# Max-unpool on one core: loading x in two transfers instead of one

## Chip, cores and metric

The kernel runs on one core of a Trainium2 chip. The metric is the device time of one execution in microseconds; "the time" below is a median over several executions. A profiled execution also gives a page and a trace; its span, from the first to the last instruction, is about 1.3 us shorter than the time. All runs compared here are at a granted clock of 1.0 (the clock of TensorE, which this kernel doesn't use).

## The reference, cut to what matters

```python
batch, channels, h, w = 16, 64, 32, 32        # x: float32, indices: 0..3
for b, c, i, j in all positions:
    idx = indices[b, c, i, j]
    output[b, c, 2*i + idx // 2, 2*j + idx % 2] = x[b, c, i, j]   # the rest stays 0
```

Each element of x goes to one of four places of a 2 x 2 cell. 1024 images of 32 x 32 become 1024 images of 64 x 64. The indices reach the device as 64-bit integers, so they are 8.4 MB against 4.2 MB of x; the output is 16.8 MB.

## The kernel before

Every partition holds eight whole images: 32 KB of x, 64 KB of indices. VectorE makes the output with `(index == k) * x` for k = 0..3, written with a stride of two, for two images at a time (for the images on either side of the cut in the indices, one at a time). Three loads are issued at the very start of the program, and four stores of 4 MB follow, each as soon as its two images are made.

```python
x_v = x.rearrange("b (ch t) h w -> (b ch) (t h w)", t=T)      # T = 8, N = 1024
...
cut = FIRST * 2 * N                                           # FIRST = 3 images
with Program(nc) as program:
    program.first(nc.sync.dma_start(out=x_t, in_=x_v).then_inc(x_in, 16))
    for half, part in enumerate((slice(0, cut), slice(cut, None))):
        program.first(
            nc.sync.dma_start(out=idx_t[:, part], in_=idx_v[:, part]).then_inc(
                idx_in[half], 16))

    nc.vector.wait_ge(x_in, 16).then_inc(x_in, -16)
    for t in range(T):
        g, k = t // G, t % G                                  # G = 2 images a store
        if t in (0, FIRST):
            half = int(t == FIRST)
            nc.vector.wait_ge(idx_in[half], 16).then_inc(idx_in[half], -16)
        ...                                                   # four operations
        if k + n == G:
            op.then_inc(made, 1)

    for g in range(NG):                                       # NG = 4
        nc.sync.wait_ge(made, g + 1)
        nc.sync.dma_start(out=out_v[g], in_=out_t[g]).then_inc(
            stored if g else stored_0, 16)
```

## Time and profile before

| | before |
|---|---|
| time, median of 3 runs | 71.66 us (71.65 to 72.0) |
| span of the profiled run | 70.2 us |
| VectorE busy | 35.6 us, 51% |
| DMA queue busy, share of 16 engines | 97.5% |
| bytes moved | 29.36 MB |

The prediction below shows the page's main lines. Two more belong beside them. The first is from the waits of the DMA-issuing SyncE, the second from the page's list of groups (busy us and mean ns of one, then the idle time just before and what ended it):

```profile
SPq L146 <- DVE out_t L133: 52.4, 4, 26.8
L133 DVE SCALAR_TENSOR_TENSOR out_t<-idx_t,x_t 128x2048 f32<-128x2048 int32 (+1 forms) x20 | 35.6, 1857 | 19.6 <-DVEq L122 19.6
```

(A q behind an engine's name means its sequencer, the part that waits and issues; L122 is the wait for the first indices.) SyncE waits 52.4 us for VectorE, and VectorE stands idle for 19.6 us before its first operation. Read alone this says that an earlier VectorE would end the kernel earlier. But SyncE only issues; what it issues stands behind the loads in the queue of the 16 DMA engines, and these are what has no gap.

### The profile page before, as it was taken

How to read it: one execution, taken by the hardware profiler on the slowest of the kernel's cores; microseconds unless marked ns; L12 is line 12 of the kernel's file. 1: busy time of each engine (PE TensorE's matmuls, PEld its weight loads, DVE VectorE, ACT ScalarE, POOL GpSimd, SP SyncE). 2: the span in 40 equal slices, each digit the busy share in tenths (PEclk: the TensorE clock that was granted, in tenths of full speed). 3: DMA queues.
4: the chain of work that ended last, by engine and by line, in shares of the span. 5: the costliest groups of instructions: out<-in, count | busy, mean ns of one | idle time of the engine just before them, and what ended most of it. 6: DMA issues, size and time to landing. Idle time of an engine off the chain costs nothing.

```text
span 70.2 us, 72 instructions
## 1 busy us (share of the span) xinstructions
DVE 35.6 (51%) x20; POOL 0.2 (0%) x4
## 2 busy tenths in 40 slices
DVE  0000000000089999999999999999999400000000
POOL 1000000000000000000000000000000000000000
DMA  9769695999988899969989696979799796969792
GB/s 280 317 299 597 299 578 243 448 448 448 597 373 373 373 513 583 397 299 485 411 355 541 299 597 299 578 317 560 336 392 504 317 578 299 597 299 560 336 504 93
DMA packets 1008, 29.36 MB, mean 418 GB/s; under 512 B 112, under 2 KB 112, under 8 KB 112
## 3 DMA queue, kind: packets, MB, share of 16 engines
q1 hardware_dynamic: 1008, 29.36, 97.5%
HBM read 12.58 MB, written 16.78 MB: 418 GB/s over the span
## 4 chain that ended last, share of the span: by engine, by line
DVE 46%; DVEq 4%; issue 1%
DVE out_t L133 46%; DVEq L183 4%
## 5 line engine op out<-in xcount | busy, mean ns | idle before, releaser
L133 DVE SCALAR_TENSOR_TENSOR out_t<-idx_t,x_t 128x2048 f32<-128x2048 int32 (+1 forms) x20 | 35.6, 1857 | 19.6 <-DVEq L122 19.6
L169 POOL MEMSET const-bfloat16-1.0<- 128x1 bf16 x1 | 0.1, 101 | 0.0
L169 POOL MEMSET const-uint8-127<- 128x1 uint8 x1 | 0.1, 101 | 0.0
L169 POOL MEMSET const-float32-0.0<- 128x1 f32 x1 | 0.1, 98 | 0.2 <-issue 0.2
L169 POOL MEMSET const-float32-1.0<- 128x1 f32 x1 | 0.1, 98 | 0.0
## 6 DMA issues: line engine op xcount, KB each, us to landing
out_dram<-out_t SPq DMA_DIRECT2D x4, 4096.0 KB, 13.8
idx_t<-in_indices_dram SPq DMA_DIRECT2D x1, 5120.0 KB, 30.6
x_t<-in_x_dram SPq DMA_DIRECT2D x1, 4096.0 KB, 12.1
idx_t<-in_indices_dram SPq DMA_DIRECT2D x1, 3072.0 KB, 19.0
```

What stands on the lines that cost most here:

```text
L133: op = nc.vector.scalar_tensor_tensor(out=o_c[:, k : k + n, :, pidx // 2, :, pidx % 2], in0=idx_c[:, t : t + n], scalar=pidx, in1=x_c[:, t ...
L169: nc = _bacc.Bacc("TRN2", target_bir_lowering=False, num_devices=1)
L183: with _tile.TileContext(nc) as tc:
```

## The change

The first image of each partition (rows of 4 KB) is loaded in a transfer of its own, the other seven (rows of 28 KB) in a second. VectorE still waits for both. As VectorE can't start sooner and the queue has no other gap, a gain could only lie in the start-up: a first transfer with short rows might get the engines going sooner.

```diff
-        program.first(nc.sync.dma_start(out=x_t, in_=x_v).then_inc(x_in, 16))
+        for part in (slice(0, N), slice(N, None)):
+            program.first(
+                nc.sync.dma_start(out=x_t[:, part], in_=x_v[:, part]).then_inc(x_in, 16)
+            )
...
-        nc.vector.wait_ge(x_in, 16).then_inc(x_in, -16)
+        nc.vector.wait_ge(x_in, 32).then_inc(x_in, -32)
```

## The prediction

> **What bounds the kernel now.** I began with the page's strip of 40 slices and its table of DMA queues, to see whether an engine or the transfers fill the span:
>
> ```profile
> span 70.2 us, 72 instructions
> DVE  0000000000089999999999999999999400000000
> DMA  9769695999988899969989696979799796969792
> DMA packets 1008, 29.36 MB, mean 418 GB/s; under 512 B 112, under 2 KB 112, under 8 KB 112
> q1 hardware_dynamic: 1008, 29.36, 97.5%
> ```
>
> VectorE works only in the middle of the span, while the one DMA queue is busy for 97.5% of what 16 engines could be. The single low slices in the DMA strip come from the way packets are booked to slices: over longer windows they vanish. So I asked for the sums of seven stretches (length, busy time of VectorE and GpSimd, granted clock, DMA share, GB/s), cut where the stages change:
>
> ```profile
> 0.00:1.03 1.03, 0.00 (x0) 0.20 (x4) 1.00 0.13 32
> 1.03:2.00 0.97, 0.00 (x0) 0.00 (x0) 1.00 1.56 473
> 2.00:3.10 1.10, 0.00 (x0) 0.00 (x0) 1.00 0.76 328
> 3.10:12.80 9.70, 0.00 (x0) 0.00 (x0) 1.00 0.99 426
> 12.80:31.30 18.50, 11.74 (x7) 0.00 (x0) 1.00 1.02 439
> 31.30:69.50 38.20, 23.86 (x14) 0.00 (x0) 1.00 0.99 425
> ```
>
> From 3.10 us to the end, through loads and stores alike, the transfers run at 425 to 439 GB/s with a share of about 1. There is no gap between the last load and the first store, nor between stores. Only the first 3.1 us differ. The chain of waits names VectorE (46%), because it follows instructions and stops at the last store's issue; it does not see that this store then stands in a queue. The timeline and the table of DMA issues show the standing:
>
> ```profile
> 19.56 35.59 DVE L133 SCALAR_TENSOR_TENSOR out_t<-idx_t,x_t 128x2048 f32<-128x2048 int32 x20 [19.56 <-DVEq L122]
> 28.49 27.03 SPq L146 DMA_DIRECT2D out_dram<-out_t  x4
> x_t<-in_x_dram SPq DMA_DIRECT2D x1, 4096.0 KB, 12.1
> idx_t<-in_indices_dram SPq DMA_DIRECT2D x1, 5120.0 KB, 30.6
> ```
>
> The second index load is issued in the first 1.4 us and lands 30.6 us after its issue, about 31.6. The first store is issued at 28.49, some 2.7 us before the first of the 16 engines finishes its loads (the completion records of that load begin at 31.19). The later stores are issued at 37.6, 46.4 and 55.2 us, while their predecessors finish at 40.9, 50.5 and 60.2, so the lead grows to 5.0 us. VectorE's first operation, which ends its wait at 19.56, waits for the first index load (line 122 is that wait), not for x: x has landed at 12.1 us.
>
> Below the views lie the trace's records of single packets. Each of the 16 engines carries 56 data packets, one for each row of a transfer: 24 KB packets take 912 ns, 32 KB packets 1213 ns and 40 KB packets 1514 ns, the same to a nanosecond or two everywhere but in the first round. Seven completion packets of 4 bytes take 9 ns each. Successive packets overlap by about 3.5 ns. The slowest engine: its first packet ends at 3.311 us, then 39 packets of 32 KB, 8 of 24 KB, 8 of 40 KB and 7 completions give 47.31 + 7.30 + 12.11 + 0.06 less 0.22 of overlap, or 66.56 us: it ends at 69.87. The last completion is seen at 70.21. So **the time is the start-up of 3.3 us, plus a fixed sum of packets, plus 0.34 us at the end**; the measured run time adds about 1.3 us outside the span (71.56 against 70.24 in the profiled run).
>
> **What the Trainium skill says.** "DMA: Bandwidth & Descriptors", section "Queues, rings and completion order": one transfer is split over up to 16 engines, and each consumes its descriptors in ring order, with no barrier between data descriptors. The trace agrees: an engine starts the first index packet straight behind its last x packet. "SBUF — State Buffer", section "The DMA setup-cost knee (why "@ 1 MiB" ≠ asymptote)", gives every transfer a fixed cost of roughly 2 us and advises the largest single transfer. Applied blindly this would charge 2 us for the new transfer; the trace of before decides against it for queued transfers, since a boundary between two of them costs one 9 ns packet. The first page's "Why a DMA increments its semaphore by 16 and not by 1" warns about transfers that share a semaphore: an intermediate count doesn't tell which bytes have landed, only the full one does. The changed kernel waits for 32, both parts in full, so nothing starts on half of x, rightly or wrongly.
>
> **The change, part by part.** It removes one transfer of 128 rows of 32 KB and adds two: 128 rows of 4 KB, then 128 of 28 KB. Bytes, the index loads, all 20 VectorE operations and all four stores are unchanged and in the same order; the comparison of the two instruction orders shows one more copy on SyncE and nothing else.
>
> 1. Packets. From 912 ns for 24 KB and 1213 for 32 KB, a byte costs 301/8192 = 0.0367 ns and a packet 912 - 903 = 9 ns besides. A 4 KB packet should take 9 + 150.5 = 160 ns, a 28 KB one 9 + 1053.5 = 1063: together 1222 against 1213. Less the overlap of 3.5 ns, each extra packet costs 5.5 ns. Per engine there are 8 more data packets and one more completion: 9 x 5.5 = 50 ns. This lies on the bounding queue: **+0.05 us**.
> 2. One more issue. Successive issues on SyncE start 0.43 to 0.48 us apart (0, 0.43 and 0.91 us), so the last index load is issued at about 1.4 us instead of 0.9. It is not needed before about 20 us: 0. The second part of x is issued at 0.43, and, by the first transfer's 1.03 to 2.00 us from issue to packets, could begin between 1.5 and 2.4. The small part occupies each engine 8 x 0.156 = 1.25 us, from about 1.8 until about 3.1. No gap: 0.
> 3. VectorE's wait for 32 instead of 16. x lands at about 12.2, the index load that VectorE really waits for at about 19.6: 0. If all loads land 0.05 us later, the operations and the stores' issues shift equally, and the lead of 2.7 us of the first store stays.
> 4. The start-up. This is the only stretch with room. The 16 first packets start between 1.03 and 2.00 us, but take 1.21 to 2.17 us instead of 1.21, and end between 2.95 and 3.31 with no relation to when they started: one that began at 1.05 ended at 2.95, one at 1.14 at 3.31. That looks like a gate which opens for all at 1.7 to 2.1 us (their ends less 1.21). A 4 KB first packet would then simply end about 1.05 us sooner and the next follow: 0.
>
> Sum: +0.05 us, so 71.66 becomes **71.7 us**.
>
> **The rivals.** A: the first packets are slow because they are large, and small ones run at the full rate from the moment they are recorded. The engine that started at 1.14 would gain 0.96 us, but the end is the slowest engine's. The last to start, at 2.00, took 1.265 us, only 0.05 too many, and ended at 69.83; without the excess, 69.77 against 69.87. So with unchanged starting times the gain is at most 0.10 us, less the 0.05: 71.6. For it speaks that first packets are slow at all; against it, that ends do not follow starts.
> B: the spread of starts, 0.97 us, is the making of descriptors, and goes with the bytes of a row. With 4 KB rows it would shrink to an eighth, all engines could start at about 1.2, and up to some 0.9 us would be saved: 70.8. Against: the issues themselves take 383 ns for 32 KB rows, 433 for 24 KB, 432 for 40 KB and 332 to 347 for the stores' 32 KB, which does not follow row size; and the gate would remain.
> C: the gate opens only when the burst of issues is over. Now the third issue ends at 1.34 us, and the gate opens at 1.73 to 2.10. A fourth issue of some 0.43 to 0.48 us moves it to about 2.2 to 2.6: 72.15. Nothing in one trace separates this from a coincidence.
> D: 4 KB pieces at a pitch of 32 KB read slower. If each small packet took twice its 160 ns, 8 x 0.16 = 1.3 us more: 73.0. The skill's "DMA: Bandwidth & Descriptors", section "Latency and other measured facts", reports losses at row pitches above 512 KiB only; the pitch here is 32 KiB, the present packets at that pitch run without loss, and no run yet shows 4 KB ones.
>
> **Range and chances.** The mainline and A lie at 71.6 to 71.7; B could take off up to 0.9, and C add 0.5. Three runs of before already spread from 71.65 to 72.0. I take 71.7 with a range of 71.3 to 72.2, which holds a partial B and all of C. Two per cent is 1.43 us: faster by that much would need more than B in full, so 0.02; slower needs D or something not thought of, so 0.03; within 2%: 0.95.
>
> **What would show it right or wrong.** In the changed profile: 1152 packets, 128 of them between 2 and 8 KB; 4 KB packets near 160 ns and 28 KB ones near 1063; DMA share about 1 from 3.1 us to the end; VectorE's first operation at 19.5 to 19.7 us, still released by the index wait; all stores issued over 2 us before the queue runs dry. If the first packets end before 1.9 us, A or B is right and the gate was the large packet; if they end after 2.4, C. A gap between the two parts of x would refute point 2, longer 4 KB packets past the first would show D. Had VectorE waited at line 120 for x, point 3 would be wrong.

## The result, and the profile after

| | before | changed |
|---|---|---|
| time, median of 6 runs | 71.69 us (71.65 to 72.0) | 71.64 us (71.56 to 71.79) |
| ratio | | 0.9986, 95% interval 0.9965 to 1.0006 |
| span of the profiled run | 70.2 us | 70.3 us |

A ratio is the mean time of one kernel's fast runs over that of the other's in the same rounds, so it is not quite the ratio of the medians. The time is the same.

The page of the changed kernel, packets and queue, then its DMA issues (KB each, us from issue to landing):

```profile
span 70.3 us, 73 instructions
DMA  4997997999988899969989796979999796969793
DMA packets 1153, 29.36 MB, mean 418 GB/s; under 512 B 129, under 2 KB 129, under 8 KB 257
q1 hardware_dynamic: 1152, 29.36, 97.7%
idx_t<-in_indices_dram SPq DMA_DIRECT2D x1, 5120.0 KB, 30.3
x_t<-in_x_dram SPq DMA_DIRECT2D x1, 3584.0 KB, 11.8
x_t<-in_x_dram SPq DMA_DIRECT2D x1, 512.0 KB, 3.7
```

There are 144 packets more on the queue: 128 of 4 KB and 16 completions of 4 bytes. (The one packet more in the first count is an instruction fetch.) The queue is as busy as before. The same stretches as in the prediction:

```profile
0.00:1.03 1.03, 0.00 (x0) 0.20 (x4) 1.00 0.08 8
1.03:2.00 0.97, 0.00 (x0) 0.00 (x0) 1.00 0.78 135
2.00:3.10 1.10, 0.00 (x0) 0.00 (x0) 1.00 1.40 581
3.10:12.80 9.70, 0.00 (x0) 0.00 (x0) 1.00 1.01 433
12.80:31.30 18.50, 11.63 (x7) 0.00 (x0) 1.00 1.02 439
31.30:69.50 38.20, 23.96 (x14) 0.00 (x0) 1.00 0.99 425
```

A packet is booked to the stretch in which it starts, with all its bytes. That is why the second stretch fell from 473 to 135 GB/s and the third rose from 328 to 581: the engines now start 4 KB there instead of 32, and the difference follows. It is no sign of slower loading. From 3.1 us on little has changed: 433, 439 and 425 GB/s against 426, 439 and 425. The timeline:

```profile
0.00 0.86 SPq L111 DMA_DIRECT2D x_t<-in_x_dram  x2
0.90 0.95 SPq L115 DMA_DIRECT2D idx_t<-in_indices_dram  x2
19.67 35.59 DVE L136 SCALAR_TENSOR_TENSOR out_t<-idx_t,x_t 128x2048 f32<-128x2048 int32 x20 [19.67 <-DVEq L125]
28.59 27.03 SPq L149 DMA_DIRECT2D out_dram<-out_t  x4
```

VectorE starts at 19.67 instead of 19.56 and is still released by line 125, the wait for the first indices, not by line 120, the wait for x. Everything behind it is about 0.1 us later.

**A measure for the start-up.** To compare it between traces I add up, over the 16 engines, the usual durations, less the overlap of 3.5 ns each, of the packets that they had done by 6 us (of one under way, the share done), divide by 16 and take this from 6 us. The result is the moment at which, on average, the engines would have had to begin at their full pace: below, "flow begins". Beside it stand the end of an engine's last packet, as the mean of the 16 and the slowest, and the "late stalls": the mean excess per engine, over their usual duration, of packets that start after 6 us. The trace doesn't name a packet's engine; it follows from which packet ends where the next begins. All are worked out from the packet records of the traces.

| trace | first rows | flow begins | late stalls | mean end | slowest end |
|---|---|---|---|---|---|
| before | 32 KB | 1.88 us | 0.01 us | 69.66 us | 69.87 us |
| before, again | 32 KB | 1.96 | 0.01 | 69.74 | 69.99 |
| changed | 4 KB | 1.78 | 0.12 | 69.72 | 69.96 |
| changed, again | 4 KB | 1.81 | 0.05 | 69.67 | 69.94 |

The means of the two traces each: flow begins 0.13 us earlier (1.92 to 1.79). What remains of the mean end when start and late stalls are taken off is 67.77 in both traces before, and 67.83 and 67.82 in the changed ones: 0.05 us more for the additional packets. The late stalls cost 0.08 us more; most of that is 40 KB packets near 29.3 us (0.10 and 0.03 us an engine in the two traces). The sum is nil: 69.70 and 69.70.

### The profile page after: what moved, and what is told of

Read it like the earlier page. It is cut to its first block, busy times and chain, and to the rows that moved or that the text cites. A ratio compares the mean times of both kernels' runs of the same rounds, so it can differ in the third digit from the quotient of the medians.

```text
span 70.3 us, 73 instructions
## 1 busy us (share of the span) xinstructions
DVE 35.6 (51%) x20; POOL 0.2 (0%) x4
## 4 chain that ended last, share of the span: by engine, by line
DVE 46%; DVEq 4%; issue 1%
DVE out_t L136 46%; DVEq L186 4%
```

## The experiments

Twelve further runs were made (three of them repeats), each timed in rounds with the kernel before on the same chip. All gave correct results. The theory at the outset: the DMA engines bound the time, a packet more costs 5.5 ns and nothing else, and the only thing that could be won is a part of the start-up. The edits of the runs with eight transfers, with a tiny first one, with the large part first and with ScalarE are shown against the changed kernel; the others against the kernel before, unless another is named. Where a cut in an edit leaves something out, three dots stand.

### The two kernels again

No edit.

> The kernel before, against itself, to have the noise of times and of the start-up in a second trace. All theories: ratio 1.000 within 0.2%, 1008 packets, all 32 KB packets but the first round at 1213 ns. The first packets should again end at about 2.9 to 3.3 us whatever their start, if a gate that opens for all engines at 1.7 to 2.1 us is a property of this program; if the ends spread anew by more than 0.3 us, the start-up of one trace is chance, and differences of 0.1 to 0.2 us between single traces carry nothing.

Measured: 71.67 us, ratio 0.9991 (0.9968 to 1.0015). The first packets ended at 2.77 to 3.44 us; the prediction's trace had 2.95 to 3.31. The ends of a single engine are thus partly chance, and the slowest engine of one trace carries nothing; the mean over 16 engines moved by 0.08 us between the two traces, and differences below that are not read. By the expectation's own yardstick (ends that spread anew by more than 0.3 us) the start-up of one trace is chance, so what is said of it below rests on several traces that agree.

> The changed kernel again. Theory 1 (the split costs 9 extra packets per engine at 5.5 ns, 0.05 us, and the start-up gives back up to 0.2 us of it, so the sum is nil): ratio 0.997 to 1.002, first packets ending at 1.5 to 2.2 us as in the first trace, earlier on average by about 0.2 us once their length is taken off. Rival (pure chance in the start-up): first packets, less 159 ns, at 1.7 to 2.1 us as in the kernel before. In both, stalls of the 40 KB packets at 29.2 to 29.5 us, seen on ten engines in the first trace of the changed kernel (up to 361 ns), should not recur at the same size if they are chance; if they recur they belong to the change.

Measured: 71.63 us, ratio 0.999 (0.996 to 1.0021). Flow begins at 1.81 us, again outside the range of the kernel before. Stalls of 40 KB packets came again at 29.2 to 29.4 us, on three engines and up to 304 ns. In the first trace they are on seven engines by the packet records, up to 361 ns, and not on ten as the expectation has it.

### x in eight transfers

```diff
-        for part in (slice(0, N), slice(N, None)):
+        for part in (slice(k * N, (k + 1) * N) for k in range(T)):
...
-        nc.vector.wait_ge(x_in, 32).then_inc(x_in, -32)
+        nc.vector.wait_ge(x_in, 16 * T).then_inc(x_in, -16 * T)
```

> The suspected cost taken seven times further: x in eight transfers of 4 KB rows. Theory 1 (a packet costs 9 ns less 3.5 ns of overlap, nothing else): against before each engine has 56 more data packets and 7 more completions, 63 x 5.5 ns = 0.35 us, so 72.0 us, ratio 1.005; second index load issued at about 4.2 us, harmless. Rival (a transfer has a fixed cost of about 2 us that queueing does not hide): 7 x 2 = 14 us more, 86 us. Rival (issue bound: 0.47 us an issue against 1.25 us of packets): no gap expected, but if there is one, it shows as 4 KB transfers that start more than 1.3 us apart.

Measured: 72.07 us, ratio 1.0045 (1.002 to 1.0071). Its timeline and its packets:

```profile
0.00 3.88 SPq L111 DMA_DIRECT2D x_t<-in_x_dram  x8
3.92 0.95 SPq L115 DMA_DIRECT2D idx_t<-in_indices_dram  x2
20.04 35.60 DVE L136 SCALAR_TENSOR_TENSOR out_t<-idx_t,x_t 128x2048 f32<-128x2048 int32 x20 [20.04 <-DVEq L125]
DMA packets 2016, 29.36 MB, mean 415 GB/s; under 512 B 224, under 2 KB 224, under 8 KB 1248
```

Issuing goes on until 4.9 us, and yet the first parts landed at 3.1 to 3.7 us and each next one 1.3 us later. So seven transfers more cost 0.3 to 0.4 us in all, as packets do, not 14 us. What remains of the mean end after start and late stalls is 68.15 us against 67.77: 0.38 us for 63 packets. Of this 0.07 is index packets that were 4 to 5 ns slower (not counted as stalls here); the rest is 5 ns for each additional packet, where 5.5 were expected. And flow begins at 1.76 us, though ten issues stand one behind another: the prediction's rival C, the end of the burst of issues as what opens the flow, is out.

### A first transfer that is tiny

```diff
-        for part in (slice(0, N), slice(N, None)):
+        for part in (slice(0, N // 8), slice(N // 8, None)):
```

> The first transfer made so small (512-byte rows, 8 packets of about 28 ns per engine, some 0.2 us) that the second part of x, issued at 0.43 us and at the engines between about 1.5 and 2.4 us, comes too late to follow without a gap. Theory 1 with the issue latency as what opens the start-up (each transfer has its own 1.0 to 2.0 us from issue to flow): gaps of 0.1 to 0.6 us between the two parts, end later by 0.1 to 0.4 us: 71.8 to 72.1. Rival (one gate for the program at 1.7 to 2.1 us, whatever the transfers): the second part starts at full rate behind the first, 71.7.

Measured: 72.05 us, ratio 1.0045 (1.0019 to 1.0071). All but four of the 128 packets of 512 bytes start at 1.03 to 1.39 us, they take 25 to 47 ns, and the 64 KB have landed at 2.0 us. The second part, issued at 0.43, then begins at 1.5 to 2.4, and its first packets are slow, by 0.08 to 1.05 us. Flow begins at 2.29 us. Its DMA issues and three stretches:

```profile
x_t<-in_x_dram SPq DMA_DIRECT2D x1, 4032.0 KB, 12.1
x_t<-in_x_dram SPq DMA_DIRECT2D x1, 64.0 KB, 2.0
```

```profile
1.00:1.50 0.50, 0.00 (x0) 0.00 (x0) 1.00 0.43 127
1.50:2.50 1.00, 0.00 (x0) 0.00 (x0) 1.00 1.85 518
2.50:6.00 3.50, 0.00 (x0) 0.00 (x0) 1.00 0.79 341
```

Hardly anything moves before 1.5 us, and the large packets that begin after it take so long that 341 GB/s start between 2.5 and 6 us, against 449 in the kernel before. This refutes the prediction's reading that a gate for the whole program opens at 1.7 to 2.1 us. The tiny packets pass at full speed long before that, and the large transfer has its own delay: 2.29 less 0.43 is 1.86 us after its issue, as the single transfer of before had 1.88 to 1.96 after its issue at 0. So a second part must come early enough to be hidden behind the first; with 4 KB rows the first lasts long enough, with 512-byte rows it doesn't.

### A large load on idle engines in mid-run

```diff
-            program.first(
-                nc.sync.dma_start(out=idx_t[:, part], in_=idx_v[:, part]).then_inc(
-                    idx_in[half], 16
-                )
-            )
+            if half == 0:
+                nc.sync.wait_ge(x_in, 16).then_inc(x_in, -16)
+            nc.sync.dma_start(out=idx_t[:, part], in_=idx_v[:, part]).then_inc(
+                idx_in[half], 16
+            )
 
-        nc.vector.wait_ge(x_in, 16).then_inc(x_in, -16)
```

> The kernel before, but SyncE issues the index loads only when x has landed, at about 12.2 us, so that a large load starts on idle engines a second time, when HBM and engines have long been in use. If any large load on an idle queue is slow in its first packets (flow 1.75 to 2.1 us after issue, as at the start): first 24 KB packets of 1.2 to 1.9 us instead of 0.91, flow at 13.9 to 14.3, engines dry since 11.3 to 11.7: 2.6 us lost, 74.3. If the slow first packets belong to the start of the program alone: packets start 0.9 to 1.2 us after issue at 912 ns, 1.6 to 1.9 us lost, 73.4. The 2 us that a page of the skill gives as the fixed cost of a transfer would show here, where the queue is empty, if anywhere.

Measured: 74.72 us, ratio 1.0431 (1.0412 to 1.0449): the first of the two theories, with 0.4 us more. (The page that the expectation means is the Trainium skill's "SBUF — State Buffer", section "The DMA setup-cost knee (why "@ 1 MiB" ≠ asymptote)".)

```profile
12.35 0.81 SPq L113 DMA_DIRECT2D idx_t<-in_indices_dram  x2
22.05 35.60 DVE L132 SCALAR_TENSOR_TENSOR out_t<-idx_t,x_t 128x2048 f32<-128x2048 int32 x20 [22.05 <-DVEq L121]
30.98 27.03 SPq L145 DMA_DIRECT2D out_dram<-out_t  x4
```

```profile
3.10:11.00 7.90, 0.00 (x0) 0.00 (x0) 1.00 1.01 436
11.00:14.30 3.30, 0.00 (x0) 0.00 (x0) 1.00 0.38 112
14.30:31.00 16.70, 8.95 (x5) 0.00 (x0) 1.00 1.02 441
```

In the middle stretch the engines are dry, at 112 GB/s. The first index packets start at 13.3 to 14.3 us, 1.0 to 2.0 after the issue, and take up to 1.73 us instead of 0.91: the picture of the start-up, 12 us into the run. By the same measure flow begins at 14.07 us, 1.72 us after the issue; x's last packets ended at 11.62 us on average, so 2.45 us were lost there. The slow beginning is therefore no matter of the program's start; a large load that finds the queue empty has it. A further 0.38 us on average are stalls of the last 40 KB packets, just ahead of the stores; why they came here, where the store was issued no earlier before the end of the loads than in the kernel before, stays open.

### The large part first

```diff
-        for part in (slice(0, N), slice(N, None)):
+        for part in (slice(N, None), slice(0, N)):
```

> The same two transfers as in the changed kernel in the other order: seven images (28 KB rows) first, then the one. The packets are the same, so their extra cost of 0.05 us is too; only the small first transfer is taken away. Theory 1 (the small first transfer opens the flow some 0.1 us earlier and so pays for the packets): time 0.1 us above the changed kernel, 71.75, first 28 KB packets slow again (up to 2.2 us for 1.06). Rival (the start-up does not depend on the first transfer's size at all, and 0.05 us is below the noise anyway): the same time as the changed kernel, 71.65 to 71.7. The difference is at the limit of what 5 rounds resolve, so the packets of the trace count for more: the mean time at which flow opens (start of the first packet plus all excess over the usual durations) should be 1.87 to 1.97 us as in the two traces of the kernel before, and not 1.77 to 1.82.

Measured: 71.88 us, ratio 1.0034 (1.0019 to 1.0048). Flow begins at 1.93 us, as in the kernel before. The time is 0.24 us above the changed kernel's, more than the 0.1 expected, so it was run again:

> The large part first, once more. The first time it was 0.24 us above the kernel before (ratio 1.0034), where packets explain 0.05; in its trace the engines ended at 69.75 us on average, as in the kernel before (69.66 and 69.74) and the changed kernel (69.72 and 69.67), but the slowest at 70.11, 0.36 later, against 0.21 to 0.27 in those four traces. If that spread was the chance of one chip and day: ratio 1.000 to 1.002, slowest engine within 0.27 us of the mean. If putting the large part first really costs more than its packets: ratio 1.003 again, slowest engine over 0.3 us past the mean.

Measured: 71.87 us, ratio 1.0021 (1.0005 to 1.0037), flow begins at 1.96 us, and the slowest engine is 0.36 us past the mean again. Together the two runs say: with the same packets, the small part first is worth 0.15 us of mean start, and without it the split is a small loss. The rest of the 0.2 us is in the wider spread of the engines' ends, whose cause no run settles. Over all traces but the one with the tiny first part, flow begins at 1.76 to 1.81 us in the four whose first rows have 4 KB (eight parts and ScalarE among them), at 1.85 to 1.89 in the three with 12 KB (the early VectorE and the two runs after it, below), and at 1.88 to 1.96 in the six with 28 or 32 KB.

### The second part issued by ScalarE

```diff
-                nc.sync.dma_start(out=x_t[:, part], in_=x_v[:, part]).then_inc(x_in, 16)
+                (nc.scalar if part.start else nc.sync)
+                .dma_start(out=x_t[:, part], in_=x_v[:, part])
+                .then_inc(x_in, 16)
```

> The second part of x is issued by ScalarE at about the same moment as the first by SyncE, so that one engine's issues do not follow each other. If making descriptors one transfer after the other holds the start-up back, the second part would be there sooner, and 0.1 to 0.3 us could be saved: 71.4 to 71.6. If start-up belongs to the first large packets of each engine, whoever issues them: 71.6 to 71.8. If two issuers hinder each other's descriptors: a later flow, 71.8 to 72.1.

Measured: 71.73 us, ratio 1.0011 (0.9997 to 1.0025). ScalarE issues at 0.13 us, 0.3 us before SyncE's second issue would; flow begins at 1.78 us, as in the changed kernel. A second issuer brings nothing.

### VectorE 6 us earlier

x and the indices are each cut after the third image and loaded in the order x, indices, x, indices; VectorE waits for a pair at a time.

```diff
-        program.first(nc.sync.dma_start(out=x_t, in_=x_v).then_inc(x_in, 16))
         for half, part in enumerate((slice(0, cut), slice(cut, None))):
+            xpart = (slice(0, FIRST * N), slice(FIRST * N, None))[half]
+            program.first(
+                nc.sync.dma_start(out=x_t[:, xpart], in_=x_v[:, xpart]).then_inc(
+                    x_ins[half], 16))
...
-        nc.vector.wait_ge(x_in, 16).then_inc(x_in, -16)
...
+                nc.vector.wait_ge(x_ins[half], 16).then_inc(x_ins[half], -16)
                 nc.vector.wait_ge(idx_in[half], 16).then_inc(idx_in[half], -16)
```

> What a split of x could be for: the first three images of x, then the indices of these three, then the rest of both, and VectorE waits only for the first pair. VectorE then starts at about (1.57 + 3.15 MB)/0.432 us + 2 = 12.9 us instead of 19.6, and the first store is issued at about 21.8 instead of 28.5. Theory 1 (the DMA queue bounds; nothing but its packets and its start-up count): the stores only wait longer in the queue, 71.7 to 71.8, ratio 0.998 to 1.004. Rival (VectorE and the chain of waits bound, as the page's chain says): the time falls by up to 6.7 us, to 65.

Measured: 72.74 us, ratio 1.0156 (1.0141 to 1.0171). Both theories missed: nothing is won, and 1.1 us is lost.

```profile
13.54 13.44 DVE L138 SCALAR_TENSOR_TENSOR out_t<-idx_t,x_t 128x2048 f32<-128x2048 int32 x8 [13.54 <-DVEq L127]
22.47 33.01 SPq L151 DMA_DIRECT2D out_dram<-out_t  x4
25.00:28.00 3.00, 1.98 (x2) 0.00 (x0) 1.00 1.02 437
28.00:31.40 3.40, 0.00 (x0) 0.00 (x0) 1.00 0.88 253
```

VectorE starts at 13.54 and the first store is issued at 22.47. Until 28 us the loads run as ever. Then the bytes fall to 253 GB/s while the busy share stays at 0.88: not a gap, but packets that last longer. Every engine's last 40 KB packet took 2.4 to 2.6 us instead of 1.51. Two runs part the possible causes. In the first, VectorE waits for all of x, which puts the first store back where it was (the edit is against the run with the early VectorE):

```diff
-                nc.vector.wait_ge(x_ins[half], 16).then_inc(x_ins[half], -16)
+                if half == 0:
+                    for s in x_ins:
+                        nc.vector.wait_ge(s, 16).then_inc(s, -16)
```

> The run with the early VectorE was 1.1 us slower, not the same, as its expectation had it: in its trace all 16 engines spent some 1.0 us too long on the last rows of the second index load, at 29.4 us, just ahead of the first store, which had stood in the queue since 22.5 us. This run keeps its order of loads (three images of x, their indices, the rest) but lets VectorE wait for all of x, so that the first store is issued at about 28.5 us again. If standing long in the queue is what costs the 1.0 us: no stall, 71.7, as the kernel before. If the order or the number of the loads costs it: 72.7 again.

Measured: 71.71 us, ratio 1.0005 (0.9989 to 1.0021). The same two stretches as above, and the store's issue:

```profile
28.77 27.03 SPq L153 DMA_DIRECT2D out_dram<-out_t  x4
25.00:28.00 3.00, 3.00 (x2) 0.00 (x0) 1.00 1.01 437
28.00:31.40 3.40, 3.40 (x4) 0.00 (x0) 1.00 0.89 383
```

The same order and number of loads, the same busy share, 383 GB/s instead of 253. In the second, the early kernel has one extra operation of 2.2 us (as in the next experiment) ahead of its first:

> The run with the early VectorE again, with one extra operation of 2.2 us ahead of the first, so that the first store is issued at about 24.7 us, 6.5 us ahead of the end of the loads instead of 8.7. If early standing in the queue costs 1.0 us whatever its length beyond a few us: 72.7. If the cost grows with the time in the queue: 72.3 to 72.5. If only the order of loads matters: 72.7 too, which the other run of this call tells apart.

Measured: 72.82 us, ratio 1.0163 (1.0138 to 1.0188), with stalls of 1.09 us per engine on average against 1.04. Its first store:

```profile
24.58 31.14 SPq L163 DMA_DIRECT2D out_dram<-out_t  x4
```

So it is the early issue of the store that costs a full microsecond, not the order of the loads, and it costs the same at 24.6 us as at 22.5. A rival is VectorE itself, whose work moved with the store and which stands idle at 27.0 to 32.9 us in the early run. The traces speak against it: in the kernel before the 24 KB packets take 912 ns each while VectorE is idle (to 19.56 us), and in the run with the late index load packets stalled while it was busy.

### VectorE 2.2 us later

```diff
...
+            if t == 0:
+                nc.vector.scalar_tensor_tensor(
+                    out=extra.rearrange("p (m i j) -> p m i j", m=2, j=W),
+                    in0=idx_c[:, 0:2], scalar=0, in1=x_c[:, 0:2],
+                    op0=mybir.AluOpType.is_equal, op1=mybir.AluOpType.mult)
             for pidx in range(4):
```

> VectorE is given one more operation of two images (about 2.2 us, result unused) before its first, so the first store's lead over the end of the loads falls from 2.7 to 0.5 us. Theory 1 with a time from issue to flow of 1.75 to 2.1 us for any transfer on an idle queue, as seen at the start of the span: the store, issued at 30.7, flows at 32.5 to 32.8, the engines have run dry at 30.9 to 31.2, so 1.3 to 1.7 us is lost: 73.0 to 73.4. If the slow flow belongs to the first reads of HBM alone, the stores flow at 1.0 to 1.2 us from their issue, 31.7 to 31.9: 0.6 to 0.9 us lost, 72.3 to 72.6. Rival (VectorE is on the path): 2.2 us more, 73.9. Rival (never on the path): 71.7.

Measured: 72.41 us, ratio 1.0109 (1.0095 to 1.0124), inside the second theory's 72.3 to 72.6.

```profile
30.71 27.03 SPq L157 DMA_DIRECT2D out_dram<-out_t  x4
30.50:31.00 0.50, 0.50 (x2) 0.00 (x0) 1.00 0.01 0
31.00:31.50 0.50, 0.50 (x1) 0.00 (x0) 1.00 0.01 0
```

The store is issued at 30.71, and until 31.5 no data packet starts; the engines run dry for 0.39 to 1.09 us each, 0.67 on average; the stores' packets start 0.85 to 1.0 us after the issue and take 1.21 to 1.25 us from the first on. So slow first packets were seen with loads alone: in this run, the only one with a store on an idle queue, the store had none. And of the 2.2 us by which VectorE was late, 0.75 reached the end: VectorE has some 1.5 us to spare, no more.

The first store's issue and what it costs at the passage from loads to stores, by these traces (the loads end at about 31.2 us, in the run with the late index load about 2.5 us later, its stalls left out; a lead of 2.7 us by this count is one of 2.3 us over the engine that is done first):

| first store issued | lead over the end of the loads | mean loss per engine |
|---|---|---|
| 30.7 (one operation more) | 0.5 us | 0.67 us dry |
| 28.5 to 29.0 (before, changed, and the split runs) | 2.4 to 2.7 | 0 to 0.1 us |
| 31.0 (late index load) | about 2.7 | 0.38 us stalled |
| 24.6 and 22.5 (early VectorE) | 6.6 and 8.7 | 1.09 and 1.04 us stalled |

The kernel before stands at the best place of those tried.

## Why the prediction was right

The prediction was 71.7 us in a range of 71.3 to 72.2, with 0.95 on "within 2%". Measured: 71.64 us. Its steps:

- **What bounds.** Right. The stretches from 3.1 us to the end are as before, and both moves of VectorE confirm it: earlier wins nothing, later by 2.2 us costs 0.75.
- **Point 1, packets, +0.05 us.** Right. The 4 KB packets took 159 ns (160 expected), the 28 KB ones 1062 (1063); the remainder of the mean end grew by 0.05 us, and the run with eight transfers gives 5 ns a packet.
- **Point 2, the additional issue, 0.** Right. The fourth issue stood at 1.375 us (1.4 expected), and the second part followed the first. The run with 512-byte rows shows the gap that a shorter first part would have left.
- **Point 3, VectorE's wait, 0.** Right: released at 19.67 us by the indices.
- **Point 4, the start-up, 0.** The reading failed. No gate opens for all engines at 1.7 to 2.1 us: the first 4 KB packets ended at 1.51 to 2.24 us, and 512-byte packets passed in 25 to 47 ns from 1.03 us on. By the prediction's own sign (first packets that end before 1.9 us mean A or B, not the gate) it failed in eight of the 16 first packets of each changed trace. What the traces show is a delay of about 1.9 us from the issue of a large load on an idle queue to its full flow (1.7 us in mid-run), and 0.13 us less of it when the first rows are 4 KB. The term was mis-sized at 0 for a measured -0.13; that is small because the largest part of the delay stays.
- **Rival A** came near in size: at most 0.10 us less 0.05 by its working, and 0.13 less 0.05 in the means. Its mechanism, full rate from the recorded start, is not what happened: first packets of 4 KB still took up to 0.99 us. **B** is out: the first packets start over 0.8 us (1.02 to 1.82) in one trace of the changed kernel and 0.5 in the other, against 0.97 before, not over an eighth. **C** is out by the ten issues. **D** is out: 159 ns.
- **A reading that was off.** The first store is issued 2.3 us, not 2.7, before the first engine is done with its loads: that engine's last 40 KB packet ends at 30.77 us and its store packet follows at once. The 31.19 us that the prediction took is the first completion on record, 0.4 us after the engine's end. The lead still sufficed.
- **What was not foreseen** is the late stall of 40 KB packets, 0.10 and 0.03 us in the two traces of the changed kernel. With the start-up's gain left out too, the sum of +0.05 came near by luck: -0.13 and +0.08 about cancel. The time alone could not have told, as the six runs of the one kernel spread by 0.35 us and those of the other by 0.23. The stall falls where the early stores stalled too, at the passage to the stores. Whether it belongs to the change stays open: the runs with the large part first, with eight parts, and with ScalarE have nearly the same lead and do not show it.

Also open: why the first packets of a large load on an idle queue are slow, and by what means a store that waits early slows the last packets of the loads. The runs show when both happen, not how.

## What to carry to other kernels

If the DMA queue is without a gap from start-up to end, splitting a load moves only packets about: work out the packets (here 5 ns each) and the start-up, and expect no more. What still counts is where the queue is empty or passes from loads to stores: keep it from running dry (about 2.5 us for a load here, once tried), and look at when the first store is issued, since both too late and much too early cost 0.7 to 1.1 us. An instruction chain that ends in VectorE does not show VectorE to be the bound if what it releases is a store that has to queue.

## What the Trainium skill lacked or had wrong

- "SBUF — State Buffer", section "The DMA setup-cost knee (why "@ 1 MiB" ≠ asymptote)", states a fixed cost of roughly 2 us for every transfer. Behind other transfers that did not hold: seven transfers more cost 0.3 to 0.4 us together, 5 ns for each additional packet. On an empty queue a cost of that order was there: with the index loads issued at 12.35 us, when x had landed, the engines stood dry for 2.45 us on average, 0.73 before the issue and 1.72 after it.
- "DMA: Bandwidth & Descriptors", section "Latency and other measured facts", gives about 0.6 us to the first byte for transfers issued by SyncE. From the end of an issue (0.38 us) to the first packet (1.03 us) this agrees. It lacks that full flow of a large load comes later, at 1.76 to 1.96 us after the issue on average over 16 engines, while 512-byte packets pass in 25 to 47 ns from 1.03 us on.
- No page that I read says that a store issued long before the loads end slows their last packets: 1.0 to 1.1 us per engine with a lead of 6.6 to 8.7 us. With 2.4 to 2.7 it was 0 to 0.1, but 0.38 in the run with the late index load.
